# Reordering the last turn of a log-sum-exp scan, and storing its last tiles whole and in row pairs

## The chip, the cores and the metric

The kernel runs on one core of one Trainium2 chip. The metric is the time of one execution on the device in microseconds (us), as the median of several executions. A profiled execution gives the trace from which the views below are taken; its span (1249.0 us before) is some 1.8 us shorter than the measured time.

## The reference, cut to what matters

```python
def reference(x):                       # x: (8, 4096, 2048) float32
    out[:, 0, :] = x[:, 0, :]
    for t in range(1, S):
        mx = np.maximum(out[:, t - 1, :], x[:, t, :])
        out[:, t, :] = mx + np.log(np.exp(out[:, t - 1, :] - mx) + np.exp(x[:, t, :] - mx))
```

It is a running log-sum-exp along the second axis: the logarithm of a running sum of exponentials. Input and output have 268.4 MB each.

## The kernel before

The sequence is cut into 64 tiles (`NT`), numbered 0 to 63 here. A tile has 128 partitions, and each partition holds four consecutive rows (`R`) of 2048 columns, so a whole tile is 32 KB per partition and 4 MiB in all. Six tiles (`NI`) are in flight. For each tile:

- SyncE loads it; ScalarE takes Exp of its two column halves in place.
- VectorE adds up the four rows within each partition (`local`, line 232: three additions per half). TensorE multiplies the last of these rows by a triangle of ones, which gives the sum of all earlier partitions, and a second matrix carries the total to the next tile. VectorE adds the result to all four rows (`join`, line 241).
- ScalarE takes Ln of the two halves in place and issues the store on its own DMA queue.

ScalarE takes the Exps of tile n before the Lns of tile n-1. In all turns but the last, a tile is stored whole. The last turn of ScalarE, which the change concerns, reads so:

```python
                for n in range(first + 1, NT):
                    up, turn = n - 1, n - 1 - first
                    exp(n, 0)
                    if n < NT - 1:
                        exp(n, 1)
                    ln(up, 0, turn)
                    if n == NT - 1:
                        store(up, o_v[up], turn, 0)      # column half 0 of tile 62
                        exp(n, 1)
                    ln(up, 1, turn)
                    store(up, o_v[up], turn, 1 if n == NT - 1 else None)
                for h in range(2):                       # tile 63, by column halves
                    ln(NT - 1, h, NT - 1 - first)
                    store(NT - 1, o_v[NT - 1], NT - 1 - first, h)
```

The softmax here doesn't subtract the row's maximum and nothing guards it: scores larger than these inputs give would overflow.

## Time and profile before

| | before |
|---|---|
| median of the first session | 1250.87 us (1250.59 to 1250.93, 3 runs) |
| span of the profiled execution | 1249.0 us |
| VectorE / ScalarE / TensorE busy | 82% / 73% / 52% |
| transfers | 537 MB, mean 430 GB/s |
| last store: issue, landing | 1236.18 us, 1247.7 us |

Three lines of the page and two pieces of the chain of waits: the first counts DMA packets by size; the next two list stores (how many, size of each, median time from issue to landing). The last two are pieces of the chain of waits (start, duration, what).

```profile
DMA packets 20409, 537.01 MB, mean 430 GB/s; under 512 B 2096, under 2 KB 2096, under 8 KB 4144
...
out_dram<-ti ACTq DMA_DIRECT2D x62, 4096.0 KB, 44.0
out_dram<-ti ACTq DMA_DIRECT2D x4, 2048.0 KB, 12.9
```

```profile
1228.00 4.42 DVE ti L241
...
1232.54 3.62 ACT ti L142
```

A 4 MiB store takes 44 us to land, over four times the 9.7 us that its bytes need, because the queues are always full. The 2048 packets between 2 and 8 KB (4144 less 2096) are the 4 KB pieces of the four column halves. The chain ends in the last join and the last Ln, and it invites the reading that these set the end. Whether they do is the main question of this study.

### The profile page before, as it was taken

To read this page: it belongs to the slowest core of one execution; us is meant where nothing else is said; L and a number is where in the kernel's file an instruction comes from. 1 tells how busy PE (TensorE), PEld (TensorE's weight loads), DVE (VectorE), ACT (ScalarE), POOL (GpSimd) and SP (SyncE) were. 2 spreads that over 40 slices of the span, in tenths; PEclk is the share of its full clock that TensorE was granted. 3 is DMA by queue.
4 is the path that set the end of the run, shared out by engine and by line. 5 is a ranking of instruction groups with operands and counts; after the bars stand their busy time and mean duration, and the time that the engine had idled before them with its cause. 6 is when DMAs were issued, how large, how long until landed. Compare 5 with 4: busy or idle time off the path is not lost. (4 is left out here: it accounts for less than half of the span.)

```text
span 1249.0 us, 3456 instructions
## 1 busy us (share of the span) xinstructions
PE 650.8 (52%) x960; PEld 215.3 (17%) x960; DVE 1023.0 (82%) x512; ACT 907.2 (73%) x258; POOL 1.1 (0%) x8
## 2 busy tenths in 40 slices
PE   3556455554566545655455544565545564465541
PEld 1112111111112111211111111121111121111110
DVE  4999978778787787887878878778787787877873
ACT  5897866867768677686776866867768677686774
POOL 0000000000000000000000000000000000000000
PEclk9897778786887868778778786777878878678785
DMA  9999999999999999999999999999999999999998
GB/s 403 420 436 430 433 430 437 433 431 434 430 436 434 431 433 430 437 434 430 434 430 436 436 430 434 430 436 437 428 434 431 436 436 429 434 430 436 436 430 354
DMA packets 20409, 537.01 MB, mean 430 GB/s; under 512 B 2096, under 2 KB 2096, under 8 KB 4144
## 3 DMA queue, kind: packets, MB, share of 16 engines
q1 hardware_dynamic: 9360, 268.44, 49.9%
q10 hardware_dynamic: 11040, 268.44, 49.9%
q8 instruction: 7, 0.11, 0.0%
q14 instruction: 2, 0.02, 0.0%
HBM read 268.44 MB, written 268.44 MB: 430 GB/s over the span
## 5 line engine op out<-in xcount | busy, mean ns | idle before, releaser
L136 ACT ACTIVATE ti<-ti 128x4096 f32<-128x4096 f32 (+1 forms) x128 | 452.6, 3582 | 310.2 <-ACTq L59 304.2
L232 DVE TENSOR_TENSOR ti<-ti 128x1024 f32<-128x1024 f32 x384 | 464.7, 1224 | 200.0 <-ACT ti L136 191.3
L241 DVE TENSOR_TENSOR ti<-ti,ps 128x4096 f32<-128x4096 f32 x128 | 560.0, 4416 | 9.4 <-PE ps L208 9.0
L208 PE MATMUL ps<-ti,before 128*128 128x512 f32 x512 | 380.4, 895 | 342.6 <-DVE ti L232 342.1
L142 ACT ACTIVATE ti<-ti 128x4096 f32<-128x4096 f32 x128 | 455.4, 3602 | 11.5 <-PE ps L197 6.0
L197 PE MATMUL ps<-ti,last 128*128 128x512 f32 x448 | 270.6, 735 | 234.2 <-DVE ti L241 234.2
L208 PEld LDWEIGHTS ps<-ti,before 128*128 128x128 f32 x512 | 128.7, 279 | 609.0 <-DVE ti L232 500.9
L197 PEld LDWEIGHTS ps<-ti,last 128*128 128x128 f32 x448 | 86.6, 214 | 401.8 <-DVE ti L241 334.7
L159 ACT ACTIVATE ti<-ti 128x4096 f32<-128x4096 f32 x1 | 3.6, 3616 | 6.5 <-ACTq L59 6.5
L32 ACT ACT_TABLE_LOAD x1 | 1.3, 1283 | 0.8 <-PEq L274 0.8
L103 POOL TENSOR_SCALAR_AFFINE_SELECT last<-last 128x128 f32<-128x128 f32 x1 | 0.3, 296 | 0.0
L98 POOL TENSOR_SCALAR_AFFINE_SELECT before<-before 128x128 f32<-128x128 f32 x1 | 0.3, 295 | 0.1
L95 POOL MEMSET last<- 128x128 f32 x1 | 0.2, 206 | 0.0
L94 POOL MEMSET before<- 128x128 f32 x1 | 0.2, 205 | 0.5 <-SPq L77 0.5
L274 POOL MEMSET const-bfloat16-1.0<- 128x1 bf16 x1 | 0.1, 103 | 0.0
L274 POOL MEMSET const-uint8-127<- 128x1 uint8 x1 | 0.1, 103 | 0.0
L274 POOL MEMSET const-float32-0.0<- 128x1 f32 x1 | 0.1, 99 | 0.3 <-issue 0.3
L274 POOL MEMSET const-float32-1.0<- 128x1 f32 x1 | 0.1, 99 | 0.0
## 6 DMA issues: line engine op xcount, KB each, us to landing
ti<-in_x_dram SPq DMA_DIRECT2D x63, 4096.0 KB, 38.4
out_dram<-ti ACTq DMA_DIRECT2D x62, 4096.0 KB, 44.0
out_dram<-ti ACTq DMA_DIRECT2D x4, 2048.0 KB, 12.9
ti<-in_x_dram SPq DMA_DIRECT2D x2, 2048.0 KB, 9.7
```

The source lines that it names most:

```text
L32: nc.scalar.preload_act_table_set("natural_log_exp_and_others")
L94: g.memset(before[:], 1.0).then_inc(ones, 1)
L98: g.affine_select(out=before[:], in_=before[:], compare_op=mybir.AluOpType.is_ge, fill=0.0, base=-1, pattern=[[1, P]], channel_multiplier= ...
L103: g.affine_select(out=last[:], in_=last[:], compare_op=mybir.AluOpType.is_ge, fill=0.0, base=-(P - 1), pattern=[[0, P]], channel_multiplier=1,
L136: act.activation(t[:, rows, half(h)], t[:, rows, half(h)], ACT.Exp).then_inc(exps[h], 1)
L142: act.activation(t[:, :, half(h)], t[:, :, half(h)], ACT.Ln)._wait_ge(carried[h], turn + 1).then_inc(logs, 1)
L159: act.activation(ti[0][:, 0:2, :], ti[0][:, 0:2, :], ACT.Exp)
L197: m = pe.matmul(ps[(n + 1) % 2][:, sl], last[:], ti[n % NI][:, R - 1, sl], start=True, stop=False, skip_group_check=True,)
L208: m = pe.matmul(ps[n % 2][:, sl], before[:], ti[n % NI][:, R - 1, sl], start=n % NBLK == 0, stop=True, skip_group_check=True,)
L232: a = dve.tensor_add(t[:, r, half(h)], t[:, r - 1, half(h)], t[:, r, half(h)])
L241: dve.tensor_add(t[:, :, half(h)], t[:, :, half(h)], ps[n % 2][:, half(h)].unsqueeze(1).to_broadcast([P, R, HALF]),)._wait_ge(ahead[h], n ...
L274: nc = _bacc.Bacc("TRN2", target_bir_lowering=False, num_devices=1)
```

## The change

Its intent is to end the last turn sooner. Both Exps of the last tile come first, so that VectorE can join earlier. Tile 62 goes out whole, and tile 63 in two pairs of rows: 16 KB in one piece per partition, in place of the 4 KB pieces of a column half. The cuts leave out the same change of `store` and `settle` in the loop.

```diff
+    LAST = [slice(0, 2), slice(2, R)]
...
-                def ln(n, h, turn):
+                def ln(n, h, turn, rows=slice(0, R)):
...
-                def store(n, dst, turn, h=None):
-                    cols = slice(0, D) if h is None else half(h)
-                    act.wait_ge(logs, 2 * turn + (2 if h is None else h + 1))
+                def store(n, dst, done, rows=slice(0, R)):
+                    act.wait_ge(logs, done)
                     act.dma_start(
-                        out=dst[:, :, cols], in_=ti[n % NI][:, :, cols]
+                        out=dst[:, rows, :], in_=ti[n % NI][:, rows, :]
                     ).then_inc(stored[n % NI], 16)
...
                 for n in range(first + 1, NT):
-                    up, turn = n - 1, n - 1 - first
-                    exp(n, 0)
-                    if n < NT - 1:
-                        exp(n, 1)
-                    ln(up, 0, turn)
-                    if n == NT - 1:
-                        store(up, o_v[up], turn, 0)
-                        exp(n, 1)
-                    ln(up, 1, turn)
-                    store(up, o_v[up], turn, 1 if n == NT - 1 else None)
-                for h in range(2):
-                    ln(NT - 1, h, NT - 1 - first)
-                    store(NT - 1, o_v[NT - 1], NT - 1 - first, h)
+                    for h in range(2):
+                        exp(n, h)
+                    for h in range(2):
+                        ln(n - 1, h, n - 1 - first)
+                    store(n - 1, o_v[n - 1], 2 * (n - first))
+                turn = NT - 1 - first
+                ln(NT - 1, 0, turn)
+                done = 2 * turn + 1
+                for rows in LAST:
+                    ln(NT - 1, 1, turn, rows)
+                    done += 1
+                    store(NT - 1, o_v[NT - 1], done, rows)
```

More of the change, by code (lines that the diff above doesn't have):

```diff
@@ L126, in _ @@
                 for n in range(NT - NI, NT):
-                    take(sp, stored[n % NI], 32 if n >= NT - 2 else 16)
+                    take(sp, stored[n % NI], 16 * (len(LAST) if n == NT - 1 else 1))
             @block.scalar
@@ L138, in exp, with settle @@
                     ).then_inc(exps[h], 1)
-                def ln(n, h, turn):
+                def ln(n, h, turn, rows=slice(0, R)):
                     t = ti[n % NI]
                     act.activation(
-                        t[:, :, half(h)], t[:, :, half(h)], ACT.Ln
+                        t[:, rows, half(h)], t[:, rows, half(h)], ACT.Ln
                     )._wait_ge(carried[h], turn + 1).then_inc(logs, 1)
-                def store(n, dst, turn, h=None):
-                    cols = slice(0, D) if h is None else half(h)
-                    act.wait_ge(logs, 2 * turn + (2 if h is None else h + 1))
+                def store(n, dst, done, rows=slice(0, R)):
+                    act.wait_ge(logs, done)
                     act.dma_start(
-                        out=dst[:, :, cols], in_=ti[n % NI][:, :, cols]
+                        out=dst[:, rows, :], in_=ti[n % NI][:, rows, :]
                     ).then_inc(stored[n % NI], 16)
-                def settle(turns):
+                def settle(turns, done):
                     take(act, carried[0], turns)
                     take(act, carried[1], turns)
-                    take(act, logs, 2 * turns)
+                    take(act, logs, done)
                 take(act, top, 16)
@@ L168, in _ @@
                         ln(n - 1, 1, n - 1)
-                        store(n - 1, o_v[bass.ds(j * NI + (n - 1), 1)][0], n - 1)
-                    settle(NI)
+                        store(n - 1, o_v[bass.ds(j * NI + (n - 1), 1)][0], 2 * n)
+                    settle(NI, 2 * NI)
                 first = turns * NI
                 for n in range(first + 1, NT):
-                    up, turn = n - 1, n - 1 - first
-                    exp(n, 0)
-                    if n < NT - 1:
-                        exp(n, 1)
-                    ln(up, 0, turn)
-                    if n == NT - 1:
-                        store(up, o_v[up], turn, 0)
-                        exp(n, 1)
-                    ln(up, 1, turn)
-                    store(up, o_v[up], turn, 1 if n == NT - 1 else None)
-                for h in range(2):
-                    ln(NT - 1, h, NT - 1 - first)
-                    store(NT - 1, o_v[NT - 1], NT - 1 - first, h)
-                settle(NT - first)
+                    for h in range(2):
[10 more added lines that the diff above has]
+                    store(NT - 1, o_v[NT - 1], done, rows)
+                settle(NT - first, done)
             @block.tensor
```

## The prediction

> **What bounds the kernel now.** I read the overall page first: busy shares, slices, queues.
>
> ```profile
> span 1249.0 us, 3456 instructions
> PE 650.8 (52%) x960; PEld 215.3 (17%) x960; DVE 1023.0 (82%) x512; ACT 907.2 (73%) x258; POOL 1.1 (0%) x8
> ...
> DMA  9999999999999999999999999999999999999998
> ...
> HBM read 268.44 MB, written 268.44 MB: 430 GB/s over the span
> ```
>
> No compute engine is over 82%, and the DMA row is full in 39 of 40 slices. The kernel moves each byte of x in once and of the output out once, 536.9 MB, and 536.9 MB at 430 GB/s is the whole span. So the transfers are the bound, and only two things can move the time: the rate of the bytes, or time at either end in which the queues are not full. The change touches the last turn only. The question is therefore how the last 40 us are filled. The stretches of time, with the share of busy DMA in the column before the last:
>
> ```profile
> 1215.00:1220.00 5.00, 3.49 (x4) 1.17 (x4) 0.92 (x1) 4.29 (x3) 0.00 (x0) 0.66 1.03 446
> 1220.00:1225.00 5.00, 1.19 (x2) 0.68 (x3) 4.92 (x4) 3.48 (x1) 0.00 (x0) 0.75 0.91 391
> 1225.00:1230.00 5.00, 2.59 (x4) 0.50 (x2) 5.00 (x2) 1.79 (x1) 0.00 (x0) 0.50 1.00 411
> 1230.00:1235.00 5.00, 0.00 (x0) 0.00 (x0) 2.41 (x1) 4.29 (x2) 0.00 (x0) 0.50 1.03 424
> 1235.00:1240.00 5.00, 0.00 (x0) 0.00 (x0) 0.00 (x0) 1.15 (x1) 0.00 (x0) 0.50 1.02 420
> 1240.00:1245.00 5.00, 0.00 (x0) 0.00 (x0) 0.00 (x0) 0.00 (x0) 0.00 (x0) 0.50 0.87 355
> 1245.00:1249.00 4.00, 0.00 (x0) 0.00 (x0) 0.00 (x0) 0.00 (x0) 0.00 (x0) 0.50 0.04 14
> ```
>
> The DMA stays full until about 1244 us, although ScalarE, VectorE and TensorE are done by 1236. The compute of the last tile runs beside a backlog of stores. I then took ScalarE's timeline (start, duration), because the change reorders it:
>
> ```profile
> 1203.27 0.35 ACTq L149 DMA_DIRECT2D out_dram<-ti  x1
> 1208.53 3.62 ACT L136 ACTIVATE ti<-ti 128x4096 f32<-128x4096 f32 x1 [5.29 <-ACTq L59]
> 1212.05 3.60 ACT L142 ACTIVATE ti<-ti 128x4096 f32<-128x4096 f32 x1
> 1215.68 0.63 ACTq L149 DMA_DIRECT2D out_dram<-ti  x1
> 1216.36 3.62 ACT L136 ACTIVATE ti<-ti 128x4096 f32<-128x4096 f32 x1 [0.71 <-ACT ti L142]
> 1219.88 3.60 ACT L142 ACTIVATE ti<-ti 128x4096 f32<-128x4096 f32 x1
> 1223.51 0.54 ACTq L149 DMA_DIRECT2D out_dram<-ti  x1
> 1228.21 3.62 ACT L142 ACTIVATE ti<-ti 128x4096 f32<-128x4096 f32 x1 [4.73 <-PEq L59]
> 1231.86 0.54 ACTq L149 DMA_DIRECT2D out_dram<-ti  x1
> 1232.54 3.62 ACT L142 ACTIVATE ti<-ti 128x4096 f32<-128x4096 f32 x1 [0.71 <-PEq L59]
> 1236.18 0.54 ACTq L149 DMA_DIRECT2D out_dram<-ti  x1
> ```
>
> Counting tiles 0 to 63, the five stores are tile 61 whole, then the column halves 62a, 62b, 63a, 63b. The view of the output tensor, asked for each issue alone, gives the time to landing: 24.6, 17.2, 14.3, 10.9 and 11.5 us. Issue plus that gives the landings: 1227.9, 1232.9, 1237.8, 1242.8, 1247.7. **Their distances are 5.0, 4.9, 5.0 and 4.9 us, whatever the distance of the issues** (7.8, 8.4, 4.3 us). So the four halves stood in one queue without a gap. The last was issued 6.6 us before its predecessor had landed. The last store's issue does not set the end; the queue does. The chain of waits seems to say otherwise (it ends in the last join and the last Ln), but it covers only 0.7% of the span and follows instructions, not transfers.
>
> **Which engine of the 16 sets the end.** The landing records in the trace hold 16 times for each store, one per DMA engine. Tile 61's are spread over 1223.7 to 1225.6 us for fifteen of them, and one is at 1227.9; the last store's over 1243.7 to 1245.5 and one at 1247.7. One engine lags by 2.2 us, and its last four intervals are the 4.9 to 5.0 us above. It works without a pause to the end.
>
> **What the Trainium skill says.**
> - DMA: Bandwidth & Descriptors, section Where 436 GB/s comes from: a ceiling of 435 GB/s for the 16 ports. The trace agrees: 433 GB/s in steady stretches.
> - The same page, section Queues, rings and completion order: a copy is spread over the rings of up to 16 engines, and each engine takes the descriptors of a ring in order. The trace agrees, with 16 landings per store and the lagging engine late in each of them.
> - ScalarE: Activation LUTs, section What ACT_TABLE_LOAD costs: an ACTIVATE with immediate operands takes 186 ns + 0.833 ns per element, thus 3.60 us for 4096 elements per partition (the rows above have 3.60 to 3.62) and 1.89 us for 2048 (the timeline has 3.71 us for two at the start, 1.86 each). Its section on table sets has Exp and Ln in one set; the page has one table load. So the new order of Exp and Ln costs no load.
> - Perfetto Trace Analysis, section DMA Optimizations: larger transfers are better, below 2 KB the overhead is significant. No packet here is that small. What the trace shows for 4 KB I work out below.
>
> **The change, part by part.**
>
> (1) *Packets.* A column half is made of 4 KB pieces (1024 floats of one row). A whole tile has 32 KB per partition, a row pair 16 KB. In the trace's packet records a 32 KB packet takes 1213 ns, a 4 KB packet 159 ns with a little overlap, and the 16 KB packets of the first two loads have a median of 611 ns. The lagging engine took 9.7 us for each whole tile (between the landings of tiles 60 and 61) and 4.95 us per column half, 9.9 per tile. For tile 62 the change thus saves 19.8/2 - 9.7 = 0.2 us. A tile in row pairs takes 16 x 0.611 = 9.8 us plus its completion writes, so tile 63 saves about 0.1 us. Sum: **0.2 to 0.3 us off the end**, because this engine is busy without a break.
>
> (2) *Later first store.* Tile 62's first half went out at 1215.7. Now ScalarE does Exp at 1208.53 and, one 3.52 us step later each, Exp at 1212.05, Ln at 1215.57 and Ln at 1219.1, which ends at 1222.7. The whole tile is issued there, **7.0 us later than its first half before and 0.8 us earlier than its second**. Is it late for the queue? The engines reach the end of tile 61 at 1223.7 to 1225.6, the lagging one at 1227.9. From the first load's issue to its first packet the trace shows 1.0 us, so descriptors stand ready at about 1223.7. The earliest engines may lose a few tenths, and they have 2 to 4 us to spare at the end. The lagging engine has 4 us of slack. Cost: 0 at the end.
>
> (3) *Earlier compute of the last tile.* The second Exp now ends at 1215.7 in place of 1220.0. VectorE: two groups of three adds, 3.75 us each, from 1212.2 to 1219.7; then two joins of 4.37 us each, 1219.7 to 1228.4. Before they ended at 1232.4, so that is 4.0 us gained. ScalarE: Ln of the first half 1224.1 to 1227.7; Ln of two rows of the second half 1228.5 to 1230.4; store; 0.7 us later (the gap shown above between store and next activation) Ln of the other two rows, 1231.1 to 1233.0; last store at 1233.0. That is **3.2 us earlier than 1236.18**. But tile 62 keeps the lagging engine till 1237.6 and the first pair till 1242.5, so the last pair waits in the queue for 9 us. Worth at the end: 0.
>
> (4) *Instructions.* One activation more (1.9 us for each of two in place of 3.6 for one, with a 0.7 us issue between them), one store less. All on ScalarE, which is not on the path.
>
> Sum: the lagging engine goes 1227.9 + 9.7 + 9.8 = 1247.4 in place of 1247.7, and what follows the last landing (1249.0 - 1247.7 = 1.3 us) stays. Change -0.2 to -0.3 us on 1250.87: **about 1250.6 us**.
>
> **Rivals.**
> - *The end hangs on the last store's issue.* Then all 3.2 us of part 3 show, and the time is about 1247.7. For it: the chain of waits ends in the last Ln. Against it: landings at even distances and an unbroken backlog. I give it 5%.
> - *The queue runs dry before tile 62.* The first store met its first packet only some 4 us after its issue, when load backlog was on the same engines. If the like happened here, descriptors would come at 1222.7 + 0.35 + 4.5 = 1227.6, all engines would wait, and the fifteen would end near 1247, beside the lagging one. Even then the end moves by less than 1 us; with a further delay, 1251 to 1252. I give a visible loss 15%.
> - *The lag itself shifts.* If the lagging engine's extra 2.2 us comes from something that the new program does less or more of, the end moves with it, at most to the other engines' 1245.5 (2.2 us off). 10%.
>
> **Range and chances.** The three runs of before lie within 0.34 us, but another session may differ by a little more than my effect. I take 1250.6 with a range of 1249.3 to 1251.8, which covers the small loss of the second rival and part of the third. Two per cent is 25 us: the whole stretch that the change can touch, from the first moved instruction to the end, is 40 us, of which the DMA is busy 36. So within 2% is nearly certain: faster 0.01, same 0.985, slower 0.005.
>
> **What would show it.** Right: the last store issued near 1233 us and landing some 14 us later; tile 62's whole store issued near 1222.7 and landing near 1237.6; the last joins ending near 1228.4; the share of busy DMA at 0.9 or above until 1243. Wrong: a stretch of idle DMA around 1223 to 1228 beyond a microsecond (second rival), a last landing less than 12 us after the issue with a gap before it (first rival), or the late engine's lag other than 2.2 us (third).

## The result, and the profile after

| | before | after |
|---|---|---|
| median, same session | 1250.78 us (1250.59 to 1250.93, 4 runs) | 1250.49 us (1250.44 to 1250.60, 4 runs) |
| span of the profiled execution | 1249.0 us | 1248.7 us |
| issue of the last store | 1236.18 us | 1234.11 us |
| last landing | 1247.7 us | 1247.3 us |

The medians differ by 0.29 us, which is 0.02%. The stated ratio is 0.9998 with a 95% interval of 0.9981 to 1.0015. A ratio is the mean time of one kernel's runs over that of the other's of the same rounds, so it isn't quite the ratio of the medians quoted here. Its interval, some 2 us to either side, does not separate the two kernels. That the 0.3 us is real rests on the traces and on the same sign in several sessions below. Executions over 1.5% slower than the fastest of the same kernel are left out of the means.

The page after: the count of packets, and the stores.

```profile
DMA packets 18729, 537.01 MB, mean 430 GB/s; under 512 B 2080, under 2 KB 2080, under 8 KB 2080
...
out_dram<-ti ACTq DMA_DIRECT2D x63, 4096.0 KB, 41.4
out_dram<-ti ACTq DMA_DIRECT2D x2, 2048.0 KB, 12.0
```

The packets of 4 KB are gone, and four stores of 2 MB have become one of 4 MB and two of 2 MB. ScalarE's timeline after (start, duration, engine, line, what; L136 is Exp, L142 Ln, L148 a store):

```profile
1204.47 0.35 ACTq L148 DMA_DIRECT2D out_dram<-ti  x1
1209.70 7.12 ACT L136 ACTIVATE ti<-ti 128x4096 f32<-128x4096 f32 x2 [5.26 <-ACTq L60]
1216.73 7.11 ACT L142 ACTIVATE ti<-ti 128x4096 f32<-128x4096 f32 x2
1223.87 0.34 ACTq L148 DMA_DIRECT2D out_dram<-ti  x1
1225.51 3.62 ACT L142 ACTIVATE ti<-ti 128x4096 f32<-128x4096 f32 x1 [1.67 <-PEq L60]
1229.84 1.91 ACT L142 ACTIVATE ti<-ti 128x2048 f32<-128x2048 f32 x1 [0.71 <-PEq L60]
1231.78 0.34 ACTq L148 DMA_DIRECT2D out_dram<-ti  x1
1232.17 1.91 ACT L142 ACTIVATE ti<-ti 128x2048 f32<-128x2048 f32 x1 [0.42 <-ACT ti L142]
1234.11 0.34 ACTq L148 DMA_DIRECT2D out_dram<-ti  x1
```

The second Exp now follows the first. The last store goes out 2.1 us earlier than the 1236.18 of before, although this execution reached its last Exps 1.2 us later (1209.70 against 1208.53). Stretches of time after (the share of busy DMA is the column before the last, GB/s the last):

```profile
1220.00:1225.00 5.00, 3.11 (x6) 0.89 (x4) 4.78 (x2) 3.84 (x2) 0.00 (x0) 0.85 0.97 419
1225.00:1230.00 5.00, 0.00 (x0) 0.00 (x0) 4.72 (x2) 3.77 (x2) 0.00 (x0) 0.83 1.01 433
1230.00:1235.00 5.00, 0.00 (x0) 0.00 (x0) 0.00 (x0) 3.66 (x2) 0.00 (x0) 0.50 0.91 390
1235.00:1240.00 5.00, 0.00 (x0) 0.00 (x0) 0.00 (x0) 0.00 (x0) 0.00 (x0) 0.50 1.00 426
1240.00:1245.00 5.00, 0.00 (x0) 0.00 (x0) 0.00 (x0) 0.00 (x0) 0.00 (x0) 0.50 0.85 360
1245.00:1249.00 4.00, 0.00 (x0) 0.00 (x0) 0.00 (x0) 0.00 (x0) 0.00 (x0) 0.50 0.03 12
```

Compute ends earlier, but the DMA is as full as before until past 1240 us. What happened shows in the landing records of the trace, 16 per store, one per DMA engine. The times are in us; "fifteen" gives the first and the last of the other engines.

| | before: fifteen | lagging | after: fifteen | lagging |
|---|---|---|---|---|
| tile 61 | 1223.7 to 1225.6 | 1227.90 | 1224.0 to 1225.6 | 1227.88 |
| tile 62 | 1233.7 to 1235.5 | 1237.82 | 1234.8 to 1235.3 | 1237.61 |
| tile 63, first piece | 1238.6 to 1240.5 | 1242.73 | 1239.7 to 1240.2 | 1242.49 |
| tile 63, second piece | 1243.7 to 1245.5 | 1247.66 | 1244.6 to 1245.0 | 1247.33 |

The lagging engine starts tile 62 at the same time in both. It takes 9.92 us for tile 62 before and 9.73 after, then 4.91 and 4.93 for the halves of tile 63 before and 4.88 and 4.84 for the row pairs after. The sum is 19.76 against 19.45 us, and the spans differ by the same 0.3 us. The fastest of the fifteen took 10.8 us for tile 62 (1224.0 to 1234.8) where 9.7 are needed, so it stood idle for 1.1 us. (By the packet records eight of the fifteen paused, each for 1.1 us at most.) It ended 2.7 us before the lagging one all the same. The trace does not name the engines; that it is one and the same that lags is inferred from the even distances of the last landings.

### The profile page after: what moved, and what is told of

It reads as the page before. It is cut to its first block, busy times and chain, and to the rows that moved or that the text cites. A ratio compares the mean times of both kernels' runs of the same rounds, so it can differ in the third digit from the quotient of the medians.

```text
span 1248.7 us, 3456 instructions
## 1 busy us (share of the span) xinstructions
PE 644.1 (52%) x960; PEld 213.1 (17%) x960; DVE 1022.8 (82%) x512; ACT 907.3 (73%) x259; POOL 1.1 (0%) x8
## 5 line engine op out<-in xcount | busy, mean ns | idle before, releaser
L136 ACT ACTIVATE ti<-ti 128x4096 f32<-128x4096 f32 (+1 forms) x128 | 452.5, 3582 | 309.7 <-ACTq L60 304.4
L231 DVE TENSOR_TENSOR ti<-ti 128x1024 f32<-128x1024 f32 x384 | 464.6, 1224 | 197.3 <-ACT ti L136 188.5
L207 PE MATMUL ps<-ti,before 128*128 128x512 f32 x512 | 372.4, 878 | 347.0 <-DVE ti L231 346.9
L142 ACT ACTIVATE ti<-ti 128x4096 f32<-128x4096 f32 x129 | 455.6, 3575 | 9.9 <-PE ps L196 7.0
```

The lines of the kernel that those rows point to most:

```text
L136: act.activation(t[:, rows, half(h)], t[:, rows, half(h)], ACT.Exp).then_inc(exps[h], 1)
L142: act.activation(t[:, rows, half(h)], t[:, rows, half(h)], ACT.Ln)._wait_ge(carried[h], turn + 1).then_inc(logs, 1)
L207: m = pe.matmul(ps[n % 2][:, sl], before[:], ti[n % NI][:, R - 1, sl], start=n % NBLK == 0, stop=True, skip_group_check=True,)
L231: a = dve.tensor_add(t[:, r, half(h)], t[:, r - 1, half(h)], t[:, r, half(h)])
```

## The experiments

**Theory.** The lagging DMA engine is never without work from the landing of tile 61 to the end, so it sets the end. Of the change only the packet size counts, and neither the order of Exp and Ln nor the issue times do. **Rival I**: the issue of the last store sets the end. **Rival G**: the pause of up to fifteen engines ahead of tile 62 ate a gain. **Rival N**: the 0.3 us is noise. Medians are compared with the kernel before, which ran on the same chip. Kernels are compared only within the same rounds. Edits are against the changed kernel.

### r0_after: the changed kernel once more

> The changed kernel once more, beside the others of this call. Theory (the transfer queue of the lagging DMA engine sets the end; only the size of the packets counts): 0.3 us under the kernel before, about 1250.5 us. Rival N (the difference is noise between runs): anything within 0.3 us on either side.

Measured: 1250.64 us against 1250.94, so 0.30 us less, in another session. The sign and the size repeat, though the ranges overlap (single runs at 1252.32 here and at 1252.29 before). That speaks against rival N without settling it alone.

### r1_order: the order alone

```diff
-                    store(n - 1, o_v[n - 1], 2 * (n - first))
+                        if n == NT - 1:
+                            store(n - 1, o_v[n - 1], 2 * (n - 1 - first) + h + 1, cols=half(h))
+                    if n < NT - 1:
+                        store(n - 1, o_v[n - 1], 2 * (n - first))
...
-                for rows in LAST:
-                    ln(NT - 1, 1, turn, rows)
+                for h in range(2):
+                    ln(NT - 1, h, turn)
...
+                    store(NT - 1, o_v[NT - 1], done, cols=half(h))
```

> The new order of the Exps and Lns alone; tiles 62 and 63 are stored in column halves, as before. Theory: the order is worth nothing, the packets are again of 4 KB, so the time is that of the kernel before, +0.0 (within 0.15 us), and the lagging engine's last four intervals are 4.9 to 5.0 us. Rival I (the end hangs on when the last store is issued): the last store goes out some 2 us earlier than before, so 2 us faster. Rival G (the about 1 us in which fifteen engines waited for tile 62 ate a gain): here the first half is out before tile 61 has drained, no gap, so faster than the changed kernel.

Measured: 1250.90 us against 1250.94 before, -0.04 (the median of the five fast executions; with the slow one it would be 1250.96). The last line of ScalarE's timeline in this run:

```profile
1233.41 0.55 ACTq L148 DMA_DIRECT2D out_dram<-ti  x1
```

The last store went out 2.8 us earlier than the 1236.18 of before, and nothing was gained: rival I falls. The first half of tile 62 went out at 1220.5, before tile 61 had drained, so no engine paused, and it wasn't faster than the changed kernel: rival G falls too. The lagging engine's four intervals were 4.96, 4.93, 4.92 and 4.95 us, as expected.

### r2_packets: the packets alone

```diff
-                    for h in range(2):
-                        exp(n, h)
-                    for h in range(2):
-                        ln(n - 1, h, n - 1 - first)
+                    exp(n, 0)
+                    if n < NT - 1:
+                        exp(n, 1)
+                    ln(n - 1, 0, n - 1 - first)
+                    if n == NT - 1:
+                        exp(n, 1)
+                    ln(n - 1, 1, n - 1 - first)
```

> The old order (Exp, Ln, Exp, Ln), but tile 62 stored whole and tile 63 in row pairs. Theory: the whole gain of the change, 0.3 us, comes from the larger packets, so 0.3 us faster than before although the last store goes out about 3 us later than in the changed kernel. Rival I: no faster than before.

Measured: 1250.54 us, 0.40 less than before, and 0.10 less than r0_after. The last store's line:

```profile
1235.84 0.34 ACTq L148 DMA_DIRECT2D out_dram<-ti  x1
```

This is 2.9 us later than in r0_after (1232.95), without a loss. With the old order and the new packets the whole gain is there. With the new order and the old packets (r1_order) there is none. The traces separate the two kinds more sharply than the medians do: from the landing of tile 61 to its last landing the lagging engine takes 19.76 us in both kernels with 4 KB packets at the end (before, r1_order), and 19.42 to 19.46 us in all six with larger ones that have no gap (after, r0, r2, r4, r6, r8). The number of stores, which also fell, is a rival that was not set up as a run. It does not account for tile 63, which goes out in two stores before and after and still takes 9.84 and 9.72 us. The cause is the packets.

### r4_last_late4 and r5_last_late12: delaying the last store

Activations of no use stand ahead of the last row pair's Ln, 4 in one run and 12 in the other.

```diff
+                def delay(times):
+                    for i in range(times):
+                        act.activation(
+                            spare[:], last[:].unsqueeze(1).to_broadcast([P, 8, P]), ACT.Exp
+                        )._wait_ge(idle, i).then_inc(idle, 1)
+                    take(act, idle, times)
...
                 for rows in LAST:
+                    if rows.start:
+                        delay(12)
                     ln(NT - 1, 1, turn, rows)
```

> The changed kernel with four activations of no use (about 1.1 us each, 4.5 us together) ahead of the Ln of the last row pair, so that its store goes out near 1238.6 us instead of 1234.1. Theory: the lagging engine has work until 1242.5 and the others until 1239.7, so nothing is lost: +0.0 us (within 0.3). Rival I (the last store's issue sets the end): +4.5 us.

Measured: 1250.63 us against 1250.98, 0.35 less than before, which is where the changed kernel stands. Four activations took 4.32 us and put the store at 1238.2; nothing was lost. (The profiled execution was the longest of the four, 1251.5 us; in it the lagging engine ended tile 61 a microsecond later, at 1229.0.)

> The same with twelve (some 13.5 us): the store goes out near 1247.6, after every queue has run dry. Theory: issue 1247.6 + about 1.1 us to the first packet + 4.9 us of packets = 1253.6 for the last landing instead of 1247.3, so +6.3 us, 7.2 us less than the delay. Rival I: +13.5 us.

Measured: 1256.11 us, 5.1 over before and so 5.4 over the changed kernel, taken as 0.3 below before. The activations took 13.04 us and put the store at 1246.06, a delay of 13.1 us against r0_after. So 7.7 us of it were hidden where 7.2 were expected. The first packet began 0.84 us after the issue, by the packet records. The first engine landed 6.12 us after it; less 0.84 and the 4.88 us that a row pair takes, some 0.4 us are left from the last packet to the landing.

### r6_62_late2 and r7_62_late8: delaying tile 62

The same `delay`, ahead of the whole store of tile 62.

```diff
+                    if n == NT - 1:
+                        delay(8)
                     store(n - 1, o_v[n - 1], 2 * (n - first))
```

> The changed kernel with two such activations (2.3 us) ahead of the whole store of tile 62, which goes out near 1226.2 instead of 1223.9. Theory: fifteen engines stand idle some 2.3 us longer, the lagging one ends tile 61 at 1227.9 and gets its descriptors just in time: +0.0 to +0.3 us. Rival G (the gap ahead of tile 62 counts): +2.3 us.

Measured: 1250.55 us against 1250.98, 0.43 less than before. The store went out at 1224.94. The fifteen engines landed tile 62 at 1235.9 to 1236.1, so the earliest, which had landed tile 61 at 1223.86, paused for 2.3 us (12.05 less 9.73), and the lagging engine still took 9.74 us from tile 61 to tile 62. Rival G falls once more: the pause costs nothing.

> The same with eight (9 us): tile 62 goes out near 1233. Theory: first packets near 1234.1, and from there three transfers of 9.73 + 4.88 + 4.84 us make 1253.6 instead of 1247.3, with the lag of one engine wiped out by the common stop: +6 us, 3 us less than the delay. Rival G: +9 us.

Measured: 1256.05 us, 5.1 over before, 5.4 over the changed kernel. Stretches of time in this run:

```profile
1220.00:1225.00 5.00, 1.71 (x4) 0.40 (x3) 5.00 (x2) 4.94 (x4) 0.00 (x0) 1.00 0.76 328
1225.00:1230.00 5.00, 0.00 (x0) 0.00 (x0) 3.41 (x1) 4.87 (x5) 0.00 (x0) 0.61 0.03 13
1230.00:1235.00 5.00, 0.00 (x0) 0.00 (x0) 0.00 (x0) 4.47 (x3) 0.00 (x0) 0.50 0.74 315
```

Now the queue does run dry: 3% busy from 1225 to 1230 us. The eight activations took 8.65 us and the store went out at 1231.44, some 8.6 us later than without them. By the medians 3.2 us of that were hidden (3 expected). All sixteen engines then landed tile 62 within 0.2 us (1242.43 to 1242.59), and no engine lagged for the rest. This is the loss that rival two of the prediction feared. It starts only when the pause reaches the lagging engine.

### r3_fifteen: leaving one engine out of the last store

```diff
-                    store(NT - 1, o_v[NT - 1], done, rows)
+                    for p in ([slice(0, P)] if rows.start == 0 else [slice(0, 120), slice(120, P)]):
+                        act.wait_ge(logs, done)
+                        act.dma_start(
+                            out=o_v[NT - 1][p, rows, :], in_=ti[(NT - 1) % NI][p, rows, :]
+                        ).then_inc(stored[(NT - 1) % NI], 16)
```

> The changed kernel, but the last row pair is stored in two transfers: partitions 0 to 119, which divide over fifteen engines, and partitions 120 to 127, over eight. Theory: if the lagging engine is the one that the large transfer leaves out, it ends after the first pair, near 1242.5 us in the trace, and the others with their 2 MB share end near 1245.6: 1.5 to 1.8 us faster than the changed kernel, 1248.8. If the lagging engine is among the eight that get one more packet, +0.6 us; if it is another, the same as the changed kernel. Rival I (issue of the last store): 0.4 us slower, for the second transfer is issued that much later.

Measured: 1253.40 us, 2.5 over before and 2.8 over r0_after. This is a miss, and none of the expectations fits. The stretches of its end:

```profile
1235.00:1240.00 5.00, 0.00 (x0) 0.00 (x0) 0.00 (x0) 0.00 (x0) 0.00 (x0) 0.50 1.02 397
1240.00:1245.00 5.00, 0.00 (x0) 0.00 (x0) 0.00 (x0) 0.00 (x0) 0.00 (x0) 0.50 0.93 246
```

From 1240 to 1245 us the DMA is 93% busy but moves only 246 GB/s. In the packet records a 16 KB packet took 614 ns in the changed kernel. Here the mean is 900 to 930 ns after 1238.4 us, and the longest took 2381. So the packets get longer from about the time when the two transfers with other partition counts start to move. Also, the engine left out was not the lagging one. The packets in flight drop from sixteen to fifteen at 1238.4 us, while the lagging engine, which landed tile 62 only at 1237.55, needs 4.9 us more for the first pair. The experiment therefore neither confirms nor refutes that relieving that engine would help. Why the packets slow down was not tested.

### r8_whole: the last tile whole

```diff
-    LAST = [slice(0, 2), slice(2, R)]
+    LAST = [slice(0, R)]
```

> The changed kernel without its row pairs: the last tile, too, is stored in one transfer, issued when its last Ln has ended, near 1232.4 us. Theory: the queues have work of tile 62 until 1234.8 (fifteen engines) and 1237.6 (the lagging one), so nothing is lost, and 32 KB packets in place of 16 KB give 0.05 us: the time of the changed kernel, 0.3 us under before. Rival P (the row pairs, with a first pair that goes out early, are what made the gain): the time of the kernel before or slower.

Measured: 1250.62 us against 1250.88, 0.26 less than before. The lagging engine took 9.73 us for tile 62 and 9.69 for tile 63. The row pairs with their early first half are worth nothing: one whole store does as well, with one activation and one store fewer.

### r9_eighths and r11_last_eighths: smaller packets at the end

In the first of these runs tiles 62 and 63 are stored in eight column pieces, so packets are of 1 KB; in the second only tile 63.

```diff
-                for rows in LAST:
-                    ln(NT - 1, 1, turn, rows)
-                    done += 1
-                    store(NT - 1, o_v[NT - 1], done, rows)
+                ln(NT - 1, 1, turn)
+                done += 1
+                for cols in EIGHTHS:
+                    store(NT - 1, o_v[NT - 1], done, cols=cols)
```

> The changed kernel, but tiles 62 and 63 are stored in eight column pieces each, packets of 1 KB; a tile's eight stores go out one after the other once its Lns are done. Theory: from 154.5 ns for 4 KB and 1216 ns for 32 KB, a packet costs about 3 ns and 37 ns per KB, so 1 KB takes about 40 ns, a tile 256 x 40 = 10.3 us on an engine instead of 9.7, and two tiles make 1.1 us: about 0.8 us slower than the kernel before, 1251.7. Rival (packet size counts for nothing, the gain of the change was something else): as the changed kernel, 1250.6.

Measured: 1257.91 us, 7.0 over before, where 0.8 was expected. The timeline of ScalarE tells why:

```profile
1224.13 9.56 ACTq L148 DMA_DIRECT2D out_dram<-ti  x8
1233.74 7.12 ACT L142 ACTIVATE ti<-ti 128x4096 f32<-128x4096 f32 x2 [9.64 <-issue]
1240.89 9.49 ACTq L148 DMA_DIRECT2D out_dram<-ti  x8
```

Eight issues kept ScalarE for 9.56 us, so the Lns of tile 63 began only at 1233.7, its first store went out at 1240.9, and the queues were empty from 1239 to 1242. I had not counted the issues. The run mixes two costs and was done again without this flaw.

> The run with column eighths without its flaw: there ScalarE spent 9.6 us on issuing tile 62's eight stores and only then began tile 63's Lns. Here tile 62 goes out whole and only tile 63 in eighths, issued last, so that no engine waits for an issue. Theory (packet size on the lagging engine sets the end): in that run an eighth took that engine 1.34 us in tile 62 and all engines 1.52 us in tile 63; eight of them make 10.7 to 12.2 us from 1237.6, so the last landing is near 1248.3 to 1249.8 instead of 1247.4, and the time 0.9 to 2.4 us over the changed kernel: 1251.5 to 1253.0. Rival (packet size counts for nothing): 1250.6.

Measured: 1251.76 us against 1250.84, 0.9 over before and 1.2 over the changed kernel (0.3 below before). The lagging engine landed tile 62 at 1237.90 and the last eighth at 1248.63: 10.73 us for the tile, 1.34 per eighth, or 42 ns per packet of 1 KB. The theory's range held. On that engine a tile takes 9.7 us in 32 or 16 KB packets, 9.9 in 4 KB, and 10.7 in 1 KB.

### r10_all_halves: 4 KB packets throughout

```diff
-                        store(n - 1, o_v[bass.ds(j * NI + (n - 1), 1)][0], 2 * n)
+                        for h in range(2):
+                            store(n - 1, o_v[bass.ds(j * NI + (n - 1), 1)][0], 2 * n, cols=half(h))
```

> Every tile stored in two column halves, 4 KB packets throughout; the new order stays. Theory: 0.15 to 0.2 us per tile as at the end, 64 times, so 10 to 12 us slower than the changed kernel, 1261, if the queues stay full all the time; more if loads (32 KB packets against 4 KB) run ahead and the stores then hold up buffers. Rival: no change, as packet size is hidden. The lag of one engine: if it comes with each transfer, 64 stores more make it grow faster than the 0.17 us in 58 us of the kernel before.

Tile 63 stays in row pairs. Measured: 1289.3 us (1284.3 to 1292.5), ratio 1.0298 (1.0274 to 1.0322), so 38 us slower, over three times what the theory gave. Packets and issues of the stretch from 600 to 800 us:

```profile
q10 hardware_dynamic: 10517, 41.78, 52.1%
q1 hardware_dynamic: 1417, 41.19, 48.9%
...
ti<-in_x_dram SPq DMA_DIRECT2D x10, 4096.0 KB, 17.3
out_dram<-ti ACTq DMA_DIRECT2D x20, 2048.0 KB, 34.9
```

The DMA is full in this stretch (52.1% and 48.9%), so most of the loss is a lower rate and not an empty queue: 420 GB/s from 60 to 1200 us, against 433 in the kernel before. Not all of it: from 1260 to 1270 us the DMA is only 50% busy. So some 5 us of the 38 are an end in which the last stores wait for compute. Loads landed in 17.3 us, against 38.4 us in the kernel before, so they do run ahead of the stores. Beside loads, both kinds of packet got longer: 163 ns on average for 4 KB (159 at the end of the kernel before), 1245 ns for 32 KB (1213 in the kernel before). The size effect of the end is thus no measure of what small packets cost beside loads; what lengthens both is open. The lag did not grow with the number of stores, which the expectation had considered: from the first engine to the last, each of the last six loads landed within 0.9 to 1.9 us, and each of the last three in the kernel before within 4.0 to 4.1.

## Why the prediction was right

The time was forecast at 1250.6 us with 1249.3 to 1251.8; it is 1250.49, and the forecast difference of 0.2 to 0.3 us measured 0.29. That the time lies in the range says little, because no change at all (1250.78) would lie in it too. And no interval of the times shows a difference this small. What speaks for the prediction are the terms below, which the traces measured one by one.

- **Part 1, packets: right.** The terms were 0.2 us for tile 62 and 0.1 for tile 63. The lagging engine's intervals gave 9.92 - 9.73 = 0.19 and 9.84 - 9.72 = 0.12 us. That this is the whole effect is shown by the crossed runs r1_order (-0.04) and r2_packets (-0.40), and by the 19.76 against 19.42 to 19.46 us of the lagging engine. And it is not noise (rival N): the five experiments at the end of which the lagging engine has the large packets without a gap (r0, r2, r4, r6, r8) are 0.26 to 0.43 us under before, in three sessions, although no single interval separates them.
- **Part 2, later first store: right.** It was to go out at 1222.7 and went out at 1223.87, because this execution reached its last Exps 1.2 us later; in r0_after it was 1222.98. The first packet began 0.84 us after the issue, where 1.0 was taken. The pause of the fastest engine was 1.1 us in the profiled execution, by its later start, and 0.4 us in r0_after (10.10 us between its landings of tiles 61 and 62, less 9.73), which are the few tenths forecast. The lagging engine's slack covered both. It was put at 4 us, and of the delay in r7_62_late8 3.2 us were hidden.
- **Part 3, earlier compute: right.** The last store was to come 3.2 us earlier. It came 2.1 us earlier in the profiled execution with its later start, and 3.2 us earlier in r0_after (1232.95). The worth at the end was put at 0, and r4_last_late4 and r5_last_late12 show it: 4.3 us of delay cost nothing, and of 13.1 us some 7.7 were hidden.
- **Part 4, instructions: right as far as can be seen.** r8_whole, without the additional Ln and store, has the time of the changed kernel.
- **The rivals.** The first (the last store's issue) fell with r1_order. The second (a dry queue) occurred in a mild form on eight engines and cost nothing; r7_62_late8 shows from where it would. The third (the lag shifts) did not show in the medians: the lagging engine ended tile 61 at 1227.88 against 1227.90. But it moves single executions: in r4_last_late4's profiled one it came a microsecond later, and the time was 1251.5 instead of 1250.6.

No version beat both kernels beyond the 0.3 us: r2_packets and r8_whole stand level with the change.

## What to carry to other kernels

When transfers are the bound, read the end of the kernel from the landing of each store, not from the last instruction: here even distances between landings, while the issues were uneven, meant that the queue set the end and that earlier compute was worth nothing. In this kernel only bytes and packet sizes then counted, and of sixteen engines only the one that ended last. Keep each store in pieces as long as its layout allows, and count the issue time of many small stores on the engine that also computes.

## What the Trainium skill lacked or had wrong

- DMA: Bandwidth & Descriptors, section Latency and other measured facts, says that two of the engines are usually slower and ties this, as its best guess, to descriptors generated in software. Here all loads and stores are of the hardware kind, and yet one engine of the sixteen fell behind: in the kernel before, the last engine landed 1.3 us after the first in a load at 62 us and 4.2 us after it in a store at 1224 us. A common stop removed the lag (r7_62_late8: 0.2 us between the first and the last). Its cause stays open.
- The same page, section Issuing engines are not separate DMA queues, calls the time to initiate a DMA usually small relative to the transfer. In r9_eighths eight stores of 512 KB took 9.56 us of ScalarE, as much as the 9.7 us that a whole tile takes to move, and delayed the Lns behind them.
- The same page, section Why a DMA increments its semaphore by 16 and not by 1, tells how the number of engines follows from the outermost size, which the landing records of r3_fifteen bear out (fifteen for 120 partitions, eight for 8). It gives no cost for such a split. Here packets of 614 ns became 900 to 930 ns on average, for a reason that was not tested.
- Perfetto Trace Analysis, section DMA Optimizations, says that batching transfers of 2 KB into ones of 4 KB or 8 KB can improve throughput dramatically. It speaks of whole transfers. Here they were of 512 KB and more and only their pieces small, so this is no direct test. A lone queue of stores lost only 2% with 4 KB pieces and 10% with 1 KB against 32 KB. Beside 32 KB loads, 4 KB pieces cost the whole kernel 3% (r10_all_halves).
